# Merged evacuation of the gate and value banks, a tap moved to ScalarE, and more seven-product couples with sums made in place

## The chip, the cores and the metric

The kernel runs on one core of one Trainium2 chip. The metric is the device time of one execution in microseconds (us); lower is better. Each time is the median of several executions. TensorE (PE) does the matrix products, VectorE (DVE) and ScalarE (ACT) do elementwise work, GpSimd (POOL) a little of it, and SyncE (SP) issues nearly all transfers.

## The reference, cut to what matters

Two layers; each is a token mixer (an mLSTM, then an HGRN2) followed by the ConvGLU below, with a norm ahead of each and a residual add behind it. All is float32; 256 tokens, width 2048, inner width 5504.

```python
def conv_glu(hn, w_up, conv_w, conv_b, w_down):
    u = hn @ w_up
    a, v = jnp.split(u, 2, axis=-1)
    s = a.shape[1]
    pad = CONV_W // 2                      # CONV_W = 3
    ap = jnp.pad(a, ((0, 0), (pad, pad), (0, 0)))
    c = conv_b
    for j in range(CONV_W):
        c = c + ap[:, j:j + s] * conv_w[j]
    return (jax.nn.gelu(c, approximate=False) * v) @ w_down
...
    for layer in range(DEPTH):             # DEPTH = 2
        ...
        h = h + mix
        h = h + conv_glu(rmsnorm(h, norm_ffn_g[layer]), ffn_w_up[layer], ...)
    return rmsnorm(h, final_g)
```

## The kernel before

**Products.** Every float32 operand is split in a rounded high part and the rest: ScalarE casts (`wh`, L137), VectorE subtracts (`wl`, L138). A product of a 128x128 block of tokens by a 128x512 block of weights is then three matmuls: high by high, high by low, low by high.

**The feed-forward part** (`ffn`) works in two parts of 22 and 21 blocks of 128 inner channels. First come the "up" chunks, one for each block (kind "fm"): 16 steps of the width, two banks of PSUM, one for the gate half a and one for the value half v; each bank is 512 wide, and the second 256 columns hold the term of the low part of x. `done_up` then evacuates the two banks: for each, ScalarE copies the second half (L355), VectorE adds the first half to it (L356) and multiplies by the norm's row R (L361). VectorE makes the three taps of the convolution (middle tap L1118, side taps L1119 and L1120), ScalarE the Gelu (L1121), VectorE the product with v (L1122), and the result is split into `g` (L1124, L1125).

**The "down" chunks** (kind "st", `squares_by_seven`) take two blocks at a time, a couple, against two column blocks of 512. A plain couple is eight products, 24 matmuls. In a couple listed in `SEVEN` the 2x2 block product is made with seven (Winograd's form): C11, C12, C21 and C22 in four banks of one pool, P1, P6, P7 and P5 in four banks of the other. It needs four sums of token blocks S1 to S4 (`token_sums`, made right after the up chunk) and four sums of weight blocks T1 to T4. After the last seven-product couple `mid` adds P1, P5, P6 and P7 into the residual stream, after the last couple `done` adds the C banks. The down chunks of part 0 are d0 and d1 (columns 0 to 1023 and 1024 to 2047), of part 1 d0 alone, and the rest of part 1 is an ordinary product, d2. A chunk of part 0 has 11 couples, 0 to 10; part 1 has ten and a single block.

**The weights' sums.** While the up chunks run, `prepare` loads the weights of each couple in `STORED`, makes the four sums in three VectorE operations into two other tiles (`weight_sums`, L179, L182, L184; the tiles are `pth` for the weights and `ptl` for the sums), and stores them to a scratch tensor in memory. In the down chunk the sums come back (`T`, L197), and `combine` splits them: `th0` and `th1` by ScalarE (L209), `tl0` and `tl1` by VectorE (L210). There is one buffer each of `th0`, `th1`, `tl0` and `tl1`, and `prepare` uses the same four. A couple in `SEVEN` but not in `STORED` (couple 9 of d0 in part 0) has its sums made on the spot.

**What sets the order.** The kernel is written in program order; the compiling layer simulates a timeline and sorts each engine's instructions by it, and each engine then runs its own list strictly in that order. Transfers of the up chunks and of `prepare` are pinned to program order (`late`). Side work such as `prepare` is a generator that is stepped as products are issued (`side.tick`); a yield of 1.0 is about 1 us of products. `split_squares` makes the operands of a down chunk three pieces ahead of its use, and first steps `prepare` to its end if it isn't there yet. Buffers: 3 of `raw` (loaded weights), 4 of `wh` and `wl`, 3 of `avc`/`T` in the feed-forward part. SyncE issues loads and stores in one queue, in order.

## Time and profile before

| | |
|---|---|
| time of 3 runs | 2391.53, 2390.47, 2388.43 us; median 2390.47 us |
| the profiled execution | span 2388.5 us from its first to its last instruction; the page gives no other time of it |
| PE | 2372.4 us busy (99%), 14614 matmul records |
| DVE | 1944.1 us (81%), 3221 instructions |
| ACT | 1298.8 us (54%) |
| POOL | 189.7 us (8%) |
| transfers | 555.07 MB, mean 232 GB/s |

[...] The up chunks of part 0 of the first layer run from about 383 to 635 us of the span, d0 and d1 from 635 to 745, the up chunks of part 1 to 980, and its down chunks to about 1080. The second layer's feed-forward part has the same stages from 1677 us to the end.

### The profile page before, as it was taken

To read this page: it belongs to the slowest core of one execution; us is meant where nothing else is said; L and a number is where in the kernel's file an instruction comes from. 1 tells how busy PE (TensorE), PEld (TensorE's weight loads), DVE (VectorE), ACT (ScalarE), POOL (GpSimd) and SP (SyncE) were. 2 spreads that over 40 slices of the span, in tenths; PEclk is the share of its full clock that TensorE was granted. 3 is DMA by queue.
4 is the path that set the end of the run, shared out by engine and by line. 5 is a ranking of instruction groups with operands and counts; after the bars stand their busy time and mean duration, and the time that the engine had idled before them with its cause. 6 is when DMAs were issued, how large, how long until landed. Compare 5 with 4: busy or idle time off the path is not lost.

```text
span 2388.5 us, 37988 instructions
## 1 busy us (share of the span) xinstructions
PE 2372.4 (99%) x14614; PEld 2030.4 (85%) x14614; DVE 1944.1 (81%) x3221; ACT 1298.8 (54%) x2013; POOL 189.7 (8%) x240
## 2 busy tenths in 40 slices
PE   9999999999999999999999999999999999999998
PEld 7888888888888888888888888888888888888887
DVE  7766687988887888777888888888889888788874
ACT  7655455454564554555555555555555565454563
POOL 0100000000000000001222222220000000000000
PEclk9999999999999999999999999999999999999999
DMA  8654556988787777755554554545798888677774
GB/s 300 201 180 165 183 178 211 333 294 317 269 293 254 251 239 262 273 194 182 173 171 168 175 177 160 177 166 188 258 325 298 298 281 296 231 249 263 249 266 148
DMA packets 98789, 555.07 MB, mean 232 GB/s; under 512 B 11168, under 2 KB 11680, under 8 KB 50736
## 3 DMA queue, kind: packets, MB, share of 16 engines
q1 hardware_dynamic: 96912, 548.64, 65.6%
q0 software_dynamic: 1120, 3.21, 0.7%
q8 instruction: 114, 1.87, 0.3%
q10 hardware_dynamic: 576, 0.79, 0.1%
q14 instruction: 67, 0.55, 0.1%
HBM read 512.69 MB, written 39.91 MB: 231 GB/s over the span
## 4 chain that ended last, share of the span: by engine, by line
PE 98%; DVE 1%; issue 1%; DMA 0%; ACT 0%; SPq 0%; POOLq 0%; POOL 0%
PE mm L328 37%; PE mm L344 23%; PE mm L332 18%; PE pc L237 12%; PE mm L237 5%; PE pn L776 1%; PE py L1034 1%; PE pd L984 1%; PE pz L405 0%; PE pa L984 0%; DMA raw<-in_w_first 0%; PE S L762 0%; DVE tl L210 0%; PE pz L1055 0%; PE pa L1009 0%
## 5 line engine op out<-in xcount | busy, mean ns | idle before, releaser
L328 PE MATMUL mm<-xt,wh 128*128 128x512 f32 x3776 | 1313.4, 394 | 0.0
L137 ACT CAST wh<-raw 128x1024 fp32r<-128x1024 f32 (+1 forms) x846 | 853.5, 1019 | 693.8 <-PE mm L328 237.9
L138 DVE TENSOR_TENSOR wl<-raw,wh 128x1024 fp32r<-128x1024 f32 (+1 forms) x846 | 1004.7, 1195 | 265.1 <-ACT wh L137 257.6
L332 PE MATMUL mm<-xt,wl 128*128 128x256 f32 x3776 | 1045.9, 278 | 0.0
L328 PEld LDWEIGHTS mm<-xt,wh 128*128 128x128 f32 x3776 | 706.2, 188 | 159.4
L332 PEld LDWEIGHTS mm<-xt,wl 128*128 128x128 f32 x3776 | 709.5, 188 | 4.5 <-issue 0.4
L344 PE MATMUL mm<-wh,xt 128*128 128x512 f32 x1024 | 320.5, 391 | 3.0 <-ACT xt L350 1.3
L344 PEld LDWEIGHTS mm<-wh,xt 128*128 128x128 f32 x1024 | 191.4, 188 | 43.3 <-ACT xt L350 1.7
L344 PE MATMUL mm<-wl,xt 128*128 128x512 f32 x512 | 198.2, 391 | 0.0
L237 PE MATMUL pc<-wh,g 128*128 128x512 f32 x508 | 167.2, 389 | 0.0
L355 ACT COPY b<-mm 128x256 f32<-128x256 f32 x236 | 87.4, 370 | 122.9 <-PE mm L332 122.7
L210 DVE TENSOR_TENSOR tl<-T,th 128x1024 fp32r<-128x1024 f32 x88 | 109.9, 1264 | 38.9 <-ACT th L209 36.7
L209 ACT CAST th<-T 128x1024 fp32r<-128x1024 f32 x88 | 92.7, 1054 | 73.6 <-PE mm L237 43.5
L237 PEld LDWEIGHTS pc<-wh,g 128*128 128x128 f32 x508 | 95.4, 188 | 19.9
L344 PEld LDWEIGHTS mm<-wl,xt 128*128 128x128 f32 x512 | 96.2, 188 | 18.9
L553 POOL TENSOR_TENSOR hm<-hm,u 128x512 f32<-128x512 f32 x8 | 10.4, 1302 | 1150.9 <-DVE u L552 1150.9
L237 PE MATMUL pc<-wl,g 128*128 128x512 f32 x254 | 98.9, 389 | 0.0
L344 PE MATMUL mm<-wh,g 128*128 128x512 f32 x308 | 96.6, 392 | 0.0
L237 PE MATMUL mm<-th,sx 128*128 128x512 f32 x264 | 91.9, 390 | 0.0
L356 DVE TENSOR_TENSOR avc<-mm,b 128x256 f32<-128x256 f32 x172 | 72.0, 418 | 14.7 <-ACT b L355 14.7
L361 DVE TENSOR_TENSOR avc<-avc,R 128x256 f32<-128x256 f32 x172 | 71.9, 419 | 1.6
L976 DVE COPY kq<-QK 128x256 f32<-128x256 f32 x224 | 69.7, 336 | 0.0
(260 smaller groups left out, 2476.7 us busy)
## 6 DMA issues: line engine op xcount, KB each, us to landing
raw<-in_w_up SPq DMA_DIRECT2D x172, 1024.0 KB, 5.5
raw<-in_w_d SPq DMA_DIRECT2D x48, 1024.0 KB, 5.0
raw<-in_w_bq SPq DMA_DIRECT2D x48, 1024.0 KB, 4.9
pth<-in_w_d SPq DMA_DIRECT2D x72, 512.0 KB, 6.7
tscr<-ptl SPq DMA_DIRECT2D x72, 512.0 KB, 4.7
T<-tscr SPq DMA_DIRECT2D x72, 512.0 KB, 5.1
raw<-in_w_d SPq DMA_DIRECT2D x36, 768.0 KB, 5.2
raw<-in_w_ao SPq DMA_DIRECT2D x24, 1024.0 KB, 4.8
```

Of the source, the lines that this page charges most:

```text
L137: pin(act.copy(wh[:, :m], r))
L138: pin(dve.tensor_tensor(wl[:, :m], r, wh[:, :m].bitcast(F32), ALU.subtract))
L209: act.copy(th, t)
L210: dve.tensor_tensor(tl, t, th.bitcast(F32), ALU.subtract)
L237: pe.matmul(ps, a, b, start=id(ps) not in begun, stop=stop and i == 2)
L328: pe.matmul(ps[f], wh[:, c:c + P], x, start=k + kk == 0, stop=False)
L332: pe.matmul(ps[f][:, 0:T], wl[:, c:c + P], x[:, 0:T], start=False, stop=k + kk == ch.nk - 1)
L344: pe.matmul(ps[t], x[:, a + t * P:a + (t + 1) * P], w[:, c], start=st and i == 0, stop=sp and i == 2)
L355: act.copy(b, ps[:, T:2 * T])
L356: dve.tensor_tensor(dst, ps[:, 0:T], b, ALU.add)
L361: dve.tensor_tensor(dst, dst, R, ALU.mult)
L976: dve.tensor_copy(m[:, j].rearrange("k (m p j) -> k m p j", p=2, j=h), blocks(z, h, 0, T))
```

## The change

It has four parts.

1. The up chunk's two banks are one tile of two banks (`banks`). One ScalarE copy takes both second halves (128x512), one VectorE addition both first halves, one VectorE multiplication applies R to both. The pool of four single banks becomes a pool of two such pairs, for all users: in a down chunk P1 and P6 share one tile, P7 and P5 the other.
2. The middle tap with its bias goes from VectorE to ScalarE (an activation of kind Identity).
3. `prepare` loads the weights of a couple into one pair of tiles (`pth` and `ptl` in turn), one couple ahead, and VectorE makes the sums in place in four operations of 128x512 each, so that no second pair of tiles is needed; it then stores them. The tiles then hold T2, T3 (first tile) and T4, T1 (second tile), where before they held T1, T3 and T2, T4.
4. Of the couples, 8 a chunk in d0 and d1 of part 0 and 6 in part 1 have seven products, all of them with stored sums. Before it was 7, 6 and 6, with 6 stored in each. In part 0 the couples are 1, 2, 3, 5, 6, 7, 8 and 9 instead of 1, 2, 4, 5, 7, 8 (and 9 in d0). To save room, the token sum S4 goes into a part of `g` that a seven-product couple doesn't read (part 0) or into a tile of its own (part 1).

```diff
-SEVEN = (1, 2, 4, 5, 7, 8, 9), (1, 2, 4, 5, 7, 8), (1, 2, 4, 5, 7, 8)
-STORED = (1, 2, 4, 5, 7, 8)
+SEVEN = (1, 2, 3, 5, 6, 7, 8, 9), (1, 2, 4, 5, 7, 8)
...
-    psm = ctx.enter_context(tc.tile_pool(name="psm", bufs=4, space=PSUM))
+    psm = ctx.enter_context(tc.tile_pool(name="psm", bufs=2, space=PSUM))
...
+    def banks():
+        return psm.tile([P, 2, 512], F32, tag="mm", name="mm")
+
     def squares_by_seven(ch, fetch, ready):
 
-        psm_ = [psm.tile([P, 512], F32, tag="mm", name="mm") for _ in range(4)]
-        P1, P6, P7, P5 = psm_
+        P1, P6, P7, P5 = psm_ = [ps[:, i] for ps in (banks(), banks()) for i in range(2)]
...
-                sx, t = ch.sums(u), q[2]
-                S1, S3, S2, S4 = ((sx[:, i * P:(i + 1) * P], sx[:, 512 + i * P:512 + (i + 1) * P]) for i in range(4))
-                T1, T3, T2, T4 = (block(t[i // 2], i % 2) for i in range(4))
+                (S1, S3, S2, S4), t = ch.sums(u), q[2]
+                T1, T3, T2, T4 = (block(t[i // 2], i % 2) for i in ((3, 1, 0, 2) if u in ch.stored else range(4)))
...
-            ps = [psm.tile([P, 512], F32, tag="mm", name="mm") for _ in range(2)]
+            both = banks()
+            ps = [both[:, i] for i in range(2)]
...
-    def token_sums(mp, i, a, b, S):
+    def token_sums(mp, i, a, b, S, last=None):
...
+        act.copy(sx[:, 0:m], S[:, 0:m])
+        dve.tensor_tensor(sx[:, m:2 * m], S[:, 0:m], sx[:, 0:m].bitcast(F32), ALU.subtract)
+        if last:
+            act.copy(last[0], S[:, m:512])
+            dve.tensor_tensor(last[1], S[:, m:512], last[0].bitcast(F32), ALU.subtract)
...
     def prepare(mp, todo, period, finished):
 
-        yield 24.0
-        for src, dst in todo:
-            r, T = ([mp.tile([P, 1024], F32, tag=f"{n}{i}", name=f"p{n}") for i in range(2)] for n in ("th", "tl"))
-            for i in range(2):
-                late(r[i], src[:, i * 1024:(i + 1) * 1024])
-            yield 9.0
-            yield from weight_sums(*r, *T)
-            for i in range(2):
-                nc.sync.dma_start(dst[i], T[i])
-            yield max(1.0, period - 14.0)
+        loaded = []
+
+        def load(i):
+            if i < len(todo):
+                n = ("th", "tl")[i % 2]
+                r = [mp.tile([P, 1024], F32, tag=f"{n}{j}", name=f"p{n}") for j in range(2)]
+                for j in range(2):
+                    late(r[j], todo[i][0][:, j * 1024:(j + 1) * 1024])
+                loaded.append(r)
+
+        yield 18.0
+        load(0)
+        for i, (_, dst) in enumerate(todo):
+            yield period / 2
+            load(i + 1)
+            B11, B22, B21, B12 = (loaded[i][j // 2][:, j % 2 * 512:(j % 2 + 1) * 512] for j in range(4))
+            for x, y, out in ((B12, B22, B22), (B12, B11, B12), (B11, B22, B11), (B21, B11, B21)):
+                dve.tensor_tensor(out, x, y, ALU.subtract)
+                yield period / 8
+            for j in range(2):
+                nc.sync.dma_start(dst[:, j * 1024:(j + 1) * 1024], loaded[i][j])
         finished.append(True)
...
-                fm_scaled(ps[0], R, a)
-                fm_scaled(ps[1], R, v)
+                av = avc[:, 0:2 * T].rearrange("p (a b) -> p a b", a=2)
+                act.copy(av, ps[:, :, T:2 * T])
+                dve.tensor_tensor(av, ps[:, :, 0:T], av, ALU.add)
+                dve.tensor_tensor(av, av, R.unsqueeze(1).broadcast_to([P, 2, T]), ALU.mult)
                 cw = [col("conv_w", (layer * 3 + w) * FT + f) for w in range(3)]
-                dve.tensor_scalar(c, a, cw[1], col("conv_b", layer * FT + f), ALU.mult, ALU.add)
+                act.activation(c, a, AF.Identity, bias=col("conv_b", layer * FT + f), scale=cw[1])
...
-                side.push(prepare(box["mp"], todo, (nf * 10.4 - 24.0) / len(todo) - 1.5, finished))
+                side.push(prepare(box["mp"], todo, (nf * 10.4 - 26.0) / len(todo), finished))
...
-                chunks.append(two(w_d1[layer], 2, None, SEVEN[1]))
+                chunks.append(two(w_d1[layer], 2, None, SEVEN[0]))
```

The changed program keeps 846 `wh` casts and 846 `wl` subtractions. It has 13363 matmul instructions where the one before has 13381, 3075 VectorE instructions for 3221, 1975 ScalarE instructions for 1933, and 723 transfers in SyncE's queue for 675.

More of the change, by code (lines that the diff above doesn't have):

```diff
@@ L195, in raw @@
                     kept[u] = [temporary(ch.pool, "T") for _ in range(2)]
-                    for t, src in zip(kept[u], ch.stored[u]):
-                        nc.sync.dma_start(t, src)
+                    for i, t in enumerate(kept[u]):
+                        nc.sync.dma_start(t, ch.stored[u][:, i * 1024:(i + 1) * 1024])
             return raws.get(u)
@@ L346, in stream @@
                     k += 1
-            ch.done(ps)
+            ch.done(both if ch.paced else ps)
     def split(dst, src, gcol, pin=lambda ins: ins):
@@ L524, in slot @@
         return where.tile([P, 2 * T], F32R, tag=f"yt{j}", name=f"{name}{j}")
-    def token_sums(mp, i, a, b, S):
-        sx = mp.tile([P, 1024], F32R, tag=f"sx{i}", name="sx")
+    def token_sums(mp, i, a, b, S, last=None):
+        m = 384 if last else 512
+        sx = mp.tile([P, 2 * m], F32R, tag=f"sx{i}", name="sx")
         for i, (x, y, op) in enumerate(((a[:, P:T], b[:, P:T], ALU.add), (a[:, P:T], a[:, 0:P], ALU.subtract),
@@ L532, in token_sums @@
             dve.tensor_tensor(S[:, i * P:(i + 1) * P], x, y, op)
-        act.copy(sx[:, 0:512], S)
-        dve.tensor_tensor(sx[:, 512:1024], S, sx[:, 0:512].bitcast(F32), ALU.subtract)
-        return sx
+        act.copy(sx[:, 0:m], S[:, 0:m])
[3 more added lines that the diff above has]
+            dve.tensor_tensor(last[1], S[:, m:512], last[0].bitcast(F32), ALU.subtract)
+        return [(sx[:, i * P:(i + 1) * P], sx[:, m + i * P:m + (i + 1) * P]) for i in range(m // P)] + ([last] if last else [])
     def pair(src, nk, c0, x, sums, norm, seven, late=False):
@@ L1098, in ffn @@
         stack = ExitStack()
-        box = dict(n=3 * len(STORED) * layer)
+        box = dict(n=(2 * len(SEVEN[0]) + len(SEVEN[1])) * layer)
         chunks, pairs = [], []
@@ L1127, in go @@
                 if i % 2 and i // 2 in seven:
-                    SX[i // 2] = token_sums(mp, seven.index(i // 2), box["c"], c, avc[:, 0:2 * T])
+                    n = seven.index(i // 2)
+                    if seven is SEVEN[0]:
+                        z = GT[i - 1][:, P:T], GT[i - 1][:, T + P:2 * T]
+                    else:
+                        if n % 3 == 0:
+                            box["s4"] = mp.tile([P, 768], F32R, tag=f"sx{len(seven) + n // 3}", name="s4")
+                        z = tuple(box["s4"][:, (n % 3 * 2 + j) * P:(n % 3 * 2 + j + 1) * P] for j in range(2))
+                    SX[i // 2] = token_sums(mp, n, box["c"], c, avc[:, 0:2 * T], z)
                 box["c"] = c
@@ L1137, in prep @@
                     begin()
-                side.push(prepare(box["mp"], todo, (nf * 10.4 - 24.0) / len(todo) - 1.5, finished))
+                side.push(prepare(box["mp"], todo, (nf * 10.4 - 26.0) / len(todo), finished))
             for i in range(nf):
-                chunks.append(Chunk("fm", w_up[layer, f0 + i], KT, norm.x, done_up(f0 + i, i, GT, SX, SEVEN[2 * part]),
+                chunks.append(Chunk("fm", w_up[layer, f0 + i], KT, norm.x, done_up(f0 + i, i, GT, SX, SEVEN[part]),
                                     prep if i == 0 else None,
@@ L1145, in two @@
                 ch = pair(src, nf, c0, lambda k: GT[k], lambda u: SX[u], norm, seven)
-                for u in STORED:
+                for u in seven:
                     ch.stored[u] = tscr[box["n"]]
@@ L1152, in two @@
                 return ch
-            chunks.append(two(w_d0[layer][:, f0 * 1024:(f0 + nf) * 1024], 0, nxt if part else None, SEVEN[2 * part]))
+            chunks.append(two(w_d0[layer][:, f0 * 1024:(f0 + nf) * 1024], 0, nxt if part else None, SEVEN[part]))
             if part:
@@ L1268, in build @@
     mscr = nc.dram_tensor("mscr", (64, T), F32, kind="Internal").ap()
-    tscr = nc.dram_tensor("tscr", (6 * len(STORED), 2, P, 1024), F32, kind="Internal").ap()
+    tscr = nc.dram_tensor("tscr", (4 * len(SEVEN[0]) + 2 * len(SEVEN[1]), P, 2048), F32, kind="Internal").ap()
     with tile.TileContext(nc, schedule_with_timeline_sim=True) as tc:
```

## The prediction

> **What bounds the kernel now.** I read the page's head first, then what TensorE waited for, then the chain that ended last, and last the stretches of one feed-forward part.

> ```profile
> span 2388.5 us, 37988 instructions
> ...
> PE 2372.4 (99%) x14614; PEld 2030.4 (85%) x14614; DVE 1944.1 (81%) x3221; ACT 1298.8 (54%) x2013; POOL 189.7 (8%) x240
> ...
> PEclk9999999999999999999999999999999999999999
> ```
> ```profile
> PE mm L237 <- DVE tl L210: 0.6, 2, 0.3
> ```
> ```profile
> 2317.31 5.44 PE pc L237 x24
> ```
> ```profile
> 383.00:635.00 252.00, 252.00 (x1449) 220.00 (x1449) 220.03 (x368) 131.19 (x195) 0.70 (x1) 1.00 0.81 292
> 635.00:750.00 115.00, 114.69 (x510) 94.62 (x509) 94.25 (x102) 67.11 (x76) 7.09 (x4) 1.00 0.79 280
> ```

> TensorE is busy 99% of the span at full clock. In the seven-product chunks (L237) it waited 0.6 us in all, for `tl`. So the time is a sum of matmuls, and only two things move it: how many there are, and any new wait in TensorE's list. The chain's row gives the price of one 128x512 matmul: 5.44 / 24 = 0.2267 us. The rows by stretch (columns: time, then busy time of PE, weight loads, DVE, ACT, POOL, clock, transfer share, GB/s) show how thin the cover is: in the up chunks of part 0 (383 to 635) VectorE is busy 87%, in d0 and d1 (635 to 750) 82%.

> **Part 1 and 2, evacuation and tap.**

> ```profile
> L356 DVE TENSOR_TENSOR avc<-mm,b 128x256 f32<-128x256 f32 x172 | 72.0, 418 | 14.7 <-ACT b L355 14.7
> L361 DVE TENSOR_TENSOR avc<-avc,R 128x256 f32<-128x256 f32 x172 | 71.9, 419 | 1.6
> ...
> L1121 ACT ACTIVATE avc<-avc 128x256 f32<-128x256 f32 x86 | 35.7, 415 | 42.3 <-DVE avc L1120 42.1
> L1118 DVE TENSOR_SCALAR avc<-avc,pp 128x256 f32<-128x256 f32 x86 | 34.9, 406 | 0.0
> ...
> L559 DVE TENSOR_TENSOR hm<-hm,pc 128x512 f32<-128x512 f32 x32 | 20.9, 676 | 0.1
> ```

> VectorE loses 72.0 + 71.9 + 34.9 = 178.8 us and gains 172 operations of 0.676 us (the row of a 512-wide addition from PSUM), 116.3 us: 62 us less, 0.73 us a chunk. ScalarE takes 86 taps of about 0.415 us, 36 us more, and the merged copy saves a little. Neither is on the path: TensorE has a second pair of banks while one is evacuated, and a chunk of products lasts 252 / 22.7 = 11.1 us. On the path this is 0; without that cover it would be one copy and one addition a chunk, 86 x 1.3 = 112 us, which no wait of the profile suggests. The order is another matter: see below.

> **Part 3, the sums in place.**

> ```profile
> L179 DVE TENSOR_TENSOR ptl<-pth 128x1024 f32<-128x1024 f32 x36 | 44.0, 1223 | 26.5 <-DMA pth<-in_w_d 22.7 <-issue 3.6
> ...
> L184 DVE TENSOR_TENSOR ptl<-pth,ptl 128x512 f32<-128x512 f32 x36 | 24.6, 683 | 0.0
> ```
> ```profile
> SPq L583 <- DVE ptl L179: 80.1, 20, 7.3
> ```
> ```profile
> raw<-in_w_up SPq DMA_DIRECT2D x172, 1024.0 KB, 5.5
> ```

> Before, 36 couples cost 1.223 + 2 x 0.683 = 2.59 us each; now 44 cost 4 x 0.683 = 2.73 us: 120 for 93 us, 27 us more on VectorE. In part 0 that is 16 for 12, +12.6 us, against 22 x 0.73 = 16.0 us saved there: VectorE stays near 87%. Loading one couple ahead takes away the 22.7 us it idled for `pth`; off the path, so 0. In SyncE's queue 16 loads, 16 stores and 16 reads back of 512 KB are added. A store waits for VectorE (80.1 us in all before) and the `raw` loads behind it wait too; their cover is the two other `raw` buffers, 2 x 5.5 us of products, against a landing of 5.5 us. I cost it at 0; with the cover gone, one landing, 5.5 us.

> **Part 4, the products.** Three more couples a layer have seven products: 2 layers x 3 x 3 = 18 matmuls, 18 x 0.2267 = **-4.1 us**. TensorE has nothing else to give.

> **The new waits.** In a run of seven-product couples `th0`, `th1`, `tl0`, `tl1` have one buffer each, so a couple's sums are split only when TensorE has read the last one's.

> ```profile
> 693.27 0.39 PE L237 MATMUL mm<-th,sx 128*128 128x512 f32 x1
> ```
> ```profile
> 693.70 1.05 ACT L209 CAST th<-T 128x1024 fp32r<-128x1024 f32 x1 [0.27 <-PE mm L237]
> ```
> ```profile
> 653.98 2.36 DVE L210 TENSOR_TENSOR tl<-T,th 128x1024 fp32r<-128x1024 f32 x2 [3.61 <-ACT th L209]
> ```
> ```profile
> L210 DVE TENSOR_TENSOR tl<-T,th 128x1024 fp32r<-128x1024 f32 x88 | 109.9, 1264 | 38.9 <-ACT th L209 36.7
> ```

> The cast starts 0.43 us after the start of the last matmul that reads (693.27 to 693.70) and takes 1.05; a subtraction takes 1.22 and the second of a pair ends 2.36 - 1.22 = 1.14 later. Counted from the start of the last read of `th0`, with 0.03 for each hand-over: `th0` at 1.51, `tl0` at 2.77, `th1` at 2.57, `tl1` at 3.91. The built programs' order tells how many matmuls stand in between. Before, at least 20 stand between the last read of a tile and the first matmul of the next couple that needs the new `tl` (4.5 us): no wait. Two things end this. Tiles shared by P1/P6 and P7/P5 keep P1 of the next couple behind P6 of this one, and P7 behind P5, so fewer matmuls can be brought forward; and couples 5 to 9 follow each other. In the changed program's TensorE order, couple 9 follows couple 8 like this (last reads of 8, first of 9):

> ```
> 3654 mm_6215<-th0_6440   3655 pc_6219<-tl1_6445   3656 pc_6219<-th1_6444
> 3657 mm_6215<-th0_6483 [waits ACT]   3658 mm_6215<-tl0_6484 [waits DVE]   3659 mm_6215<-th0_6483
> 3660 mm_6216<-th1_6487 [waits ACT]   3661 pc_6219<-th1_6487   3662 mm_6216<-tl1_6488 [waits DVE]
> ```

> Couple 10 has been used up as filler ahead of 3654. Matmul 3657 has its place 3 x 0.2267 = 0.68 us after 3654 and starts at 1.51: wait 0.83. 3658 could start at 1.74 and starts at 2.77: 1.03. 3662 has its place four later, 3.68, and starts at 3.91: 0.23. Together 2.1 us, in d0 and d1 of both layers (the order is the same): **+8.4 us**.

> Couples 2 to 3 of d0: 6 matmuls stand between; the first of 3 waits 1.51 - 1.36 = 0.15, its `th1` matmul 2.57 - 1.74 = 0.83: 1.0 us, twice: **+2.0 us**. The other neighbours (3 to 5, 5 to 6, 6 to 7, 7 to 8, and part 1) have 11 to 34 before `th0` and 13 or more before `tl0` is needed, 2.9 us against 2.77: 0.

> From d0 to d1, VectorE's list after `tl1` of couple 9 (3.91) is: five evacuations, `tl0` of d1's couple 1, one more, `wl` of d1's couple 1, `tl1`, and the addition that frees P7/P5.

> ```profile
> 688.64 0.68 DVE L551 TENSOR_TENSOR hm<-hm,mm 128x512 f32<-128x512 f32 x1
> ...
> 689.23 0.68 DVE L548 TENSOR_TENSOR u<-u,mm 128x512 f32<-128x512 f32 x1
> ...
> 695.41 2.29 POOL L554 TENSOR_TENSOR hm<-hm,u 128x512 f32<-128x512 f32 x1
> ```

> An evacuation takes 0.60 (688.64 to 689.23), so `wl` ends at 3.9 + 6 x 0.60 + 2 x 1.14 = 9.8. TensorE wants it 21 matmuls after 3662, at 8.7: wait 1.1; the freed bank comes at 9.8 + 1.14 + 0.6 = 11.5, wanted 5 matmuls later at 10.9: 0.6. Together 1.7 us, twice: **+3.4 us**. POOL's additions come behind that. From d1 to the up chunks the same list leaves 1.8 us of room: 0.

> **Sum.** -4.1 + 8.4 + 2.0 + 3.4 = +9.7 us. Against the profiled span 2388.5 that is 2398.2; the median of the runs stands 2.0 above that span, so I forecast **2400 us**, 0.4% slower.

> **The transfers, as a bound.**

> ```profile
> T<-tscr SPq DMA_DIRECT2D x72, 512.0 KB, 5.1
> ```
> ```profile
> DMA to landing us min/median/max: 3.3/5.1/7.8
> ```
> ```profile
> 720.00:725.00 5.00, 2.16 (x3) 1.00 0.99 387
> ```
> ```profile
> 425.00:435.00 10.00, 10.00 (x60) 8.73 (x59) 9.34 (x15) 5.21 (x8) 0.00 (x0) 1.00 0.92 347
> ```

> A seven-product couple loads 768 + 2 x 512 KB, 1.84 MB in 21 x 0.2267 = 4.76 us, 386 GB/s, as much as the best five microseconds of d1 (387). A run of five at 347 GB/s takes 26.5 us for 23.8: 2.7 us late, in four chunks 10.7 us, less what the plain couples give back. I take 0, since d0 and d1 together need 35.7 MB in 109 us, 328 GB/s. The second `T` tile of couple 9 is loaded only once `tl0` of couple 8 frees its buffer, at the latest 11 matmuls (2.5 us) ahead of 3654, so 4.0 us before its cast could start at 1.5: at a landing of 5.1 it's up to 1.1 us late, at 7.8 up to 3.8, four times 4.4 or 15. I take 0, because that `tl0` may end earlier. [...]

> **Rivals.**

> *Only the waits from 8 to 9 show* (d0 to d1 and 2 to 3 covered, as before's own 0.6 us speaks for): 2390.5 - 4.1 + 8.4 = 2395, no measurable change.

> *Transfers bind in the long runs*: the rows above speak for it, the mean against it. 2400 + 11 = 2411.

> *The matmuls saved come through and no wait does*: 2390.5 - 4.1 = 2386.4, not slower. It needs the waits to sum to under 4.1 us, that is 8 to 9 under 1.0 us each. Against it stands the row of a cast that starts only after the read; for it, that VectorE sheds 62 us and could be earlier everywhere else.

> *The clock falls after the new waits.* It's at full in every slice, and where TensorE stops for good the row shows less:

> ```profile
> 2379.00:2388.50 9.50, 0.87 (x4) 0.38 (x2) 3.80 (x8) 2.67 (x4) 0.68 (x2) 0.69 0.60 221
> ```

> Six us of half clock behind each of four stops would cost 4 x 3 = 12 us: 2412. The longest single wait is 1.0 us. [...]

> **Chances.** The forecast as worked out 0.48; only 8 to 9, 0.20; transfers 0.20; no wait 0.05; clock 0.03; something in the up chunks not seen 0.04. What a measurement can tell from no change is about 0.2%, 4.8 us: slower beyond 2395.3 is then 0.75, within 0.20 (the case of 2395), faster 0.05. The range is 2391 to 2414: below, the case of 2395 with half its waits; above, the case of late transfers. The forecast's own range is 2396 to 2405.

> **What would show it.** Right: TensorE 4 us less of matmuls in L238, and in its waits some 14 us in L238 for `th0`/`th1` (ACT) and `tl` (DVE), at four places of about 2 us near 690 and 740 and their like in the second layer; VectorE's total some 20 us less; clock full. Wrong: no such waits, or waits in the up chunks for `wl`, or casts there and in d0 released by transfers of `T`.

## The result, and the profile after

The changed kernel takes 2429.4 us (median of 5 runs, 2426.5 to 2432.4) against the 2390.5 us of before; run beside each other the ratio is 1.0163, with a 95% interval of 1.0150 to 1.0175. It is 1.6% slower. I had forecast 2400 us, so the direction was right and 29 us were missing. The profiled execution of the changed kernel took 2427.9 us, its span is 2426.2 us, 37.7 us longer than the span shown of before.

The page's head, with the shares of the chain that ended last, then what TensorE waited for (behind the arrow the releaser, that is, the engine and tile that ended the wait; then total us, times, longest us):

```profile
span 2426.2 us, 38067 instructions
...
PE 2386.3 (98%) x14596; PEld 2030.4 (84%) x14596; DVE 1933.8 (80%) x3075; ACT 1349.0 (56%) x2055; POOL 194.2 (8%) x240
...
PE 83%; DMA 7%; DVE 6%; issue 2%; ACT 1%; SPq 0%; POOL 0%; POOLq 0%; ACTq 0%; DVEq 0%
```
```profile
PE mm L238 <- ACT th L208: 10.3, 10, 1.8
PE pd L1000 <- issue: 6.1, 3, 2.5
PE mm L238 <- DVE tl L209: 4.2, 5, 1.1
PE pc L238 <- ACT wh L136: 3.3, 3, 2.3
PE mm L238 <- ACT wh L136: 1.6, 3, 0.7
PE pc L238 <- ACT th L208: 1.4, 2, 0.7
```

The 18 matmuls are gone (14614 to 14596). But TensorE is idle 39.9 us of the span (2426.2 - 2386.3) where it was idle 16.1, and its busy time rose by 13.9 us although it has less to do, because part of it ran at half clock (three stretches of 3.4 us at a clock of 0.50), and because a matmul's record (0.39 us and more) is longer than the distance to the next start (0.2267 us), so that a part of each wait counts as busy. In the chain TensorE had 98% before; now it has 83%, and transfers and VectorE have 13%. In line 238, the seven-product products, the waits for `th`, `tl` and `wh` sum to 20.8 us. And one row has nothing to do with these chunks: 6.1 us ahead of the small `pd` products of the second mixer, with no releaser.

One row of ScalarE's waits, before and after, shows that its casts of `th` now wait for transfers of `T`:

```profile
ACT th L209 <- DMA T<-tscr: 7.1, 6, 2.0
```
```profile
ACT th L208 <- DMA T<-tscr: 21.4, 14, 3.8
```

The stretches tell where the time went. First before, then after, each with d0 and d1 of the first layer, the second mixer, and d0 and d1 of the second layer (columns as in the prediction: time, then busy time of PE, weight loads, DVE, ACT, POOL, clock, transfer share, GB/s):

```profile
635.40:747.10 111.70, 111.39 (x492) 91.71 (x491) 91.29 (x98) 65.44 (x74) 7.09 (x4) 1.00 0.79 278
...
1093.00:1679.40 586.40, 582.79 (x4988) 499.54 (x4988) 508.93 (x1003) 325.49 (x606) 142.96 (x179) 1.00 0.51 174
...
1925.00:2036.60 111.60, 111.34 (x492) 91.61 (x491) 91.38 (x98) 65.25 (x74) 7.08 (x4) 1.00 0.79 279
```
```profile
636.50:761.80 125.30, 116.21 (x482) 89.92 (x481) 94.74 (x104) 73.19 (x86) 3.00 (x2) 0.99 0.83 299
...
1107.90:1702.00 594.10, 585.90 (x4988) 501.19 (x4987) 507.46 (x1003) 326.55 (x606) 146.55 (x179) 1.00 0.51 172
...
1947.60:2073.40 125.80, 115.14 (x482) 90.08 (x481) 92.82 (x100) 71.63 (x83) 3.01 (x2) 0.99 0.82 294
```

d0 and d1 take 13.6 and 14.2 us more, 27.8 together, with 9 matmuls fewer each; the mixer takes 7.7 us more for the same products; the rest of the span adds 2.2 (0.9 at the end of the first up chunks, 1.1 in the last chunk). I added up the distances between starts of matmuls in d0 and d1, less the 0.2267 us that one is worth. Both layers together have 32.4 us of idle or slowed time there:

| place in d0 and d1, both layers | us |
|---|---|
| couple 1 of d0, waiting for `th` and for the `wh` behind it | 4.1 |
| couple 3 of d0, waiting for `th` | 6.2 |
| half clock right behind it | 3.2 |
| couple 8 to 9, four times | 8.9 |
| d0 to d1, twice | 4.5 |
| later waits for `T` or `raw` | 5.6 |

Less the 4.1 us of matmuls saved, that is 28.3, against the 27.8 by which the two stretches grew.

### The profile page after: what moved, and what is told of

Its sections match the earlier page's. It is cut to its first block, busy times and chain, and to the rows that moved or that the text cites. A ratio compares the mean times of both kernels' runs of the same rounds, so it can differ in the third digit from the quotient of the medians.

```text
span 2426.2 us, 38067 instructions
## 1 busy us (share of the span) xinstructions
PE 2386.3 (98%) x14596; PEld 2030.4 (84%) x14596; DVE 1933.8 (80%) x3075; ACT 1349.0 (56%) x2055; POOL 194.2 (8%) x240
## 4 chain that ended last, share of the span: by engine, by line
PE 83%; DMA 7%; DVE 6%; issue 2%; ACT 1%; SPq 0%; POOL 0%; POOLq 0%; ACTq 0%; DVEq 0%
PE mm L329 31%; PE mm L345 21%; PE mm L333 16%; PE pc L238 7%; PE mm L238 4%; DVE wl L137 2%; DMA T<-tscr 2%; DMA pth<-in_w_d 2%; DMA ptl<-in_w_d 1%; DVE tl L209 1%; ACT th L208 1%; PE pn L792 1%; DMA raw<-in_w_d 1%; PE py L1050 1%; PE pd L1000 1%
## 5 line engine op out<-in xcount | busy, mean ns | idle before, releaser
L209 DVE TENSOR_TENSOR tl<-T,th 128x1024 fp32r<-128x1024 f32 x100 | 120.1, 1221 | 60.8 <-ACT th L208 60.5
L238 PE MATMUL pc<-wh,g 128*128 128x512 f32 x488 | 163.3, 391 | 3.4 <-ACT wh L136 3.3
L208 ACT CAST th<-T 128x1024 fp32r<-128x1024 f32 x100 | 102.8, 1050 | 98.1 <-PE mm L238 56.3
L238 PE MATMUL mm<-th,sx 128*128 128x512 f32 x300 | 107.9, 397 | 10.6 <-ACT th L208 10.3
L238 PEld LDWEIGHTS pc<-wh,g 128*128 128x128 f32 x488 | 91.9, 188 | 24.1 <-ACT wh L136 5.1
L238 PE MATMUL pc<-wl,g 128*128 128x512 f32 x244 | 95.6, 392 | 0.1
L1136 ACT ACTIVATE avc<-avc,pp 128x256 f32<-128x256 f32 x86 | 51.7, 601 | 51.4 <-DVE avc L1134 51.0
L238 PEld LDWEIGHTS mm<-th,sx 128*128 128x128 f32 x300 | 56.9, 190 | 26.3 <-ACT th L208 14.3
L597 DVE TENSOR_TENSOR ptl<-ptl 128x512 f32<-128x512 f32 x88 | 60.4, 686 | 23.2 <-DMA ptl<-in_w_d 22.9
L597 DVE TENSOR_TENSOR pth<-pth 128x512 f32<-128x512 f32 x88 | 60.3, 685 | 21.2 <-DMA pth<-in_w_d 15.0
## 6 DMA issues: line engine op xcount, KB each, us to landing
raw<-in_w_up SPq DMA_DIRECT2D x172, 1024.0 KB, 6.3
raw<-in_w_bq SPq DMA_DIRECT2D x48, 1024.0 KB, 5.0
T<-tscr SPq DMA_DIRECT2D x88, 512.0 KB, 5.5
raw<-in_w_d SPq DMA_DIRECT2D x40, 1024.0 KB, 5.2
raw<-in_w_ao SPq DMA_DIRECT2D x24, 1024.0 KB, 4.8
pth<-in_w_d SPq DMA_DIRECT2D x44, 512.0 KB, 8.0
ptl<-in_w_d SPq DMA_DIRECT2D x44, 512.0 KB, 7.8
```

Source lines behind the costliest of these rows:

```text
L208: act.copy(th, t)
L209: dve.tensor_tensor(tl, t, th.bitcast(F32), ALU.subtract)
L238: pe.matmul(ps, a, b, start=id(ps) not in begun, stop=stop and i == 2)
L597: dve.tensor_tensor(out, x, y, ALU.subtract)
L1136: act.activation(c, a, AF.Identity, bias=col("conv_b", layer * FT + f), scale=cw[1])
```

## The experiments

Four theories stood against each other, under the letters that the expectations use. **O**: the order of TensorE's list, with tiles shared by two banks, makes the waits (the prediction's). **L**: the preparation of the weights' sums in part 0 ends too late, so SyncE issues the first loads of `T` late. **D**: the transfers can't feed runs of seven-product couples. **M**: the merged banks or the sums in place are slow by themselves. For the mixer's waits there were **F** (TensorE waits for its next block of instructions) and **C** (the change itself causes them). Every kernel is compared with the kernel before on the same chip, 2389.6 to 2390.4 us in these comparisons.

What suggested L, in rows. SyncE's first load of `T` before and after:

```profile
621.65 3.32 SPq L197 DMA_DIRECT2D T<-tscr  x2
```
```profile
635.88 0.32 SPq L196 DMA_DIRECT2D T<-tscr  x1
```

ScalarE and TensorE of the changed kernel at the start of d0 (start, time, then in brackets the idle time before and its releaser):

```profile
644.60 1.04 ACT L208 CAST th<-T 128x1024 fp32r<-128x1024 f32 x1 [1.86 <-DMA T<-tscr]
...
647.02 0.58 ACT L1132 COPY avc<-mm 128x512 f32<-128x512 f32 x1
...
661.33 2.21 ACT L208 CAST th<-T 128x1024 fp32r<-128x1024 f32 x2 [2.51 <-DMA T<-tscr]
```
```profile
645.70 0.50 PE L238 MATMUL pc<-th,g 128*128 128x512 f32 x1 [0.67 <-ACT th L208]
...
662.42 0.50 PE L238 MATMUL mm<-th,sx 128*128 128x512 f32 x1 [1.79 <-ACT th L208]
...
696.35 0.50 PE L238 MATMUL mm<-th,sx 128*128 128x512 f32 x1 [0.67 <-ACT th L208]
...
697.60 0.50 PE L238 MATMUL mm<-tl,sx 128*128 128x512 f32 x1 [0.76 <-DVE tl L209]
```

d0 starts at about 636, and the first `T` is asked for at 635.9, 14 us later than before. ScalarE, in order, sits in front of the cast of couple 1, and behind that cast wait the weights' casts and the evacuation of the last up chunk (647.02; it was at 635.29 before). The three buffers of `T` are the up chunks' too, and the last up chunk holds one of them, so the first `T` of couple 3 is asked for only at 655.4, when VectorE has read one of couple 2; it lands (has arrived) 5.8 us later, and its cast at 661.33 is what couple 3 waits for. The last two rows are the place from couple 8 to 9.

**The sums prepared faster** (early_sums).

```diff
-  prepare(box["mp"], todo, (nf * 10.4 - 26.0) / len(todo), finished)
+  prepare(box["mp"], todo, min(10.4, (nf * 10.4 - 26.0) / len(todo)), finished)
```

> Edit: the changed kernel, with the sums of the weights in part 0 prepared faster, a couple every 10.4 us of products instead of 14.3 (sixteen couples end about one up chunk earlier). Theory L (the preparation ends too late): T of couple 1 reaches d0 earlier, so the waits at the start of d0 (about 2 us for th of couple 1, 3.1 us for th of couple 3) and the half clock behind the second (1.7 us) go in both layers, 2 x 6.8 = 13.6 us; in the built order couple 7 to 8 of d0 now has three matmuls between its reads like 8 to 9, which costs 1.6 us twice: 2429 - 13.6 + 3.2 = about 2419. Theory O (the order of TensorE's list is the cause): these waits stay, 2429 + 3 = 2432. Theory D (the transfers bind): the up chunks now ask for 2.1 MB of sums beside 2.1 MB of weights in 11.1 us, 380 GB/s against a best of 387, so the up chunks of part 0 get waits for raw or wl and nothing is gained, 2429 or more.

Measured 2425.1 us, 4.3 less than the changed kernel; single runs overlap (2420.9 to 2428.7, and 2426.5 to 2432.4), so the trace has to tell. Its first load of `T`, a wait that the changed kernel doesn't have, and the five microseconds around that wait:

```profile
622.86 0.33 SPq L196 DMA_DIRECT2D T<-tscr  x1
```
```profile
1807.95 0.38 PE L333 MATMUL mm<-xt,wl 128*128 128x256 f32 x1 [0.88 <-DVE wl L137]
```
```profile
1805.00:1810.00 5.00, 4.12 (x24) 3.37 (x24) 5.00 (x8) 4.28 (x6) 0.00 (x0) 1.00 0.91 375
```

Theory L holds for the start of d0: `T` is asked for 13 us earlier, the waits of couples 1 and 3 are gone in both layers (the first wait of d0 is now at 676), and d0 with d1 are 3.2 and 5.8 us shorter, with the new waits from 7 to 8 in them. In the second layer the up chunks got four such waits for `wl` of 0.7 to 0.9 us and became 5.8 us longer, so that layer gained nothing. Theory D had named such waits, but not for what the trace shows: in the 4 us ahead of each, VectorE was busy for 3.96 us or more, and ScalarE's casts waited for `raw` for 0.8 us in that whole stage. So these waits are VectorE's, which has the sums between its other work, and not the transfers'.

**The old couples** (old_couples).

```diff
-SEVEN = (1, 2, 3, 5, 6, 7, 8, 9), (1, 2, 4, 5, 7, 8)
+SEVEN = (1, 2, 4, 5, 7, 8), tuple([1, 2, 4, 5, 7, 8])
```

> Edit: the changed kernel, with six seven-product couples a chunk (1, 2, 4, 5, 7, 8) in d0 and d1 of part 0 and in part 1, all with stored sums; merged evacuation, the tap on ScalarE and the sums in place stay. 24 matmuls more than the changed kernel, 5.4 us. Theory L and theory O both: no wait in d0 and d1 is left but 1 us at d1's start, so the time is before's plus 6 matmuls (1.4 us), 2392; if the mixer's 7.7 us (TensorE's small products waiting on nothing that the profile shows, and a half clock) come from the merged banks, 2400. Theory M (merged banks or the sums in place are themselves slow): 2405 or more, with waits in d0 and d1 for th or for banks.

Measured 2395.9 us (2394.4 to 2398.1). 33.5 us of the 39 went with two of the eight couples, although 5.4 us of matmuls came back: d0 and d1 take 112.6 and 113.2 us. The first `T` is asked for at 626.8, and at d0's start no wait for `th` is left, only one of 0.6 us for `wl` in the second layer. The time lies 4 us above the 2392 of theories L and O; the next runs say what that is.

**Merged evacuation and the tap alone, on the kernel before** (merged_alone).

```diff
-    psm = ctx.enter_context(tc.tile_pool(name="psm", bufs=4, space=PSUM))
+    psm = ctx.enter_context(tc.tile_pool(name="psm", bufs=2, space=PSUM))
-        psm_ = [psm.tile([P, 512], F32, tag="mm", name="mm") for _ in range(4)]
+        P1, P6, P7, P5 = psm_ = [ps[:, i] for ps in (banks(), banks()) for i in range(2)]
...
+                act.copy(av, ps[:, :, T:2 * T])
+                dve.tensor_tensor(av, ps[:, :, 0:T], av, ALU.add)
+                dve.tensor_tensor(av, av, R.unsqueeze(1).broadcast_to([P, 2, T]), ALU.mult)
...
+                act.activation(c, a, AF.Identity, bias=col("conv_b", layer * FT + f), scale=cw[1])
```

> Edit: the kernel before with parts 1 and 2 of the change alone (merged banks and evacuation, tap on ScalarE); sums and couples as before. As predicted: nothing on the path, 2390. Rival: the mixer between the two feed-forward parts loses its 7.7 us here too, because its chunks' banks are now freed in pairs, 2398.

Measured 2399.4 us, ratio 1.0044 (1.0029 to 1.0059). So these parts cost 9.3 us by themselves, and not in the mixer (586.9 us, before 586.4). d0 with d1 take 4.1 us more in each layer. TensorE where d0 gives way to d1 in this kernel, and ScalarE's first copy of `mid` in this kernel and before:

```profile
691.80 0.51 PE L239 MATMUL mm<-wh,g 128*128 128x512 f32 x1 [1.58 <-ACT wh L137]
693.39 0.51 PE L239 MATMUL pc<-wh,g 128*128 128x512 f32 x1 [1.09 <-DVE hm L562]
```
```profile
688.95 0.58 ACT L549 COPY u<-mm 128x512 f32<-128x512 f32 x1
```
```profile
679.42 0.59 ACT L546 COPY u<-mm 128x512 f32<-128x512 f32 x1
```

`mid` copies P1 at 688.95 instead of 679.42, and VectorE's first addition from these banks begins at 687.99 instead of 681.80: P1 now shares its tile with P6. So the evacuations that free the banks of d1 fall together with d1's first splits, TensorE waits twice, 2.7 us by these rows, and runs at half clock behind that (from 694.39 us, for 3.4 us).

**Banks of their own in the changed kernel** (single_banks).

```diff
-        P1, P6, P7, P5 = psm_ = [ps[:, i] for ps in (banks(), banks()) for i in range(2)]
+        P1, P6, P7, P5 = psm_ = [psm.tile([P, 512], F32, tag="mm", name="mm") for _ in range(4)]
...
-                act.copy(av, ps[:, :, T:2 * T])
-                dve.tensor_tensor(av, ps[:, :, 0:T], av, ALU.add)
-                dve.tensor_tensor(av, av, R.unsqueeze(1).broadcast_to([P, 2, T]), ALU.mult)
+                fm_scaled(ps[0], R, a)
+                fm_scaled(ps[1], R, v)
```

> Edit: the changed kernel with part 1 undone: four banks of their own in the pool, each evacuated by a copy, an addition and a multiplication; the tap stays on ScalarE, the sums in place and the 8, 8 and 6 couples stay. Theory O (shared tiles keep the couples' matmuls in line): in the built order 11 and 7 matmuls stand between the reads from couple 8 to 9 instead of 3, so the four waits of 2.3 us there fall to 0 in d1 and 0.7 in d0, a gain of 7.8 us, about 2421; the waits at the start of d0 stay. Theory D: the couples wait for T or raw instead, and the gain is under 3 us. If the mixer's 7.7 us come from the shared tiles, they go too, 2413.

Measured 2409.8 us, 19.6 less than the changed kernel. d0, d1 and the up chunks behind them (their products overlap, so I take them together) are 3.0 and 5.0 us shorter. These 8.0 agree with the 7.8 of theory O by luck. As it said, the waits from 8 to 9 in d1 are gone. But in d0 the stretch from couple 5 to couple 9 has 14.3 us of idle or slowed time in both layers, where the changed kernel has 7.7; its longest wait, 1.9 us at 697.9, ends with a cast that waited for `T`:

```profile
696.84 1.04 ACT L208 CAST th<-T 128x1024 fp32r<-128x1024 f32 x1 [3.17 <-DMA T<-tscr]
```

The start of d0, where theory O expected no change, has 8.1 us for 13.8, and the waits from d0 to d1 are gone. The mixer is 10.5 us shorter, more than I expected; idle_half below shows that 8.2 us can go there by the place of the instructions alone, with the tiles as they are.

**Parts 2 and 3 alone** (single_old: the last two edits together, banks of their own and the old couples).

> Edit: banks of their own and six couples a chunk (1, 2, 4, 5, 7, 8) everywhere, all with stored sums; so the kernel before with parts 2 and 3 alone (tap on ScalarE, sums in place), and without couple 9 of d0, 6 matmuls more than before (1.4 us). If parts 2 and 3 are free as predicted: 2391 to 2393, and the 4 us that the run with old couples and merged banks stands above it are the merged banks' price. If the sums in place cost by themselves: 2395 or more, with waits in d0.

Measured 2391.3 us, ratio 1.0004 (0.9995 to 1.0014). With twelve couples in part 0 the tap on ScalarE and the sums in place cost nothing, and theory M falls for them. The merged banks cost 4.6 us there (2395.9 - 2391.3), but not where they did in merged_alone: by the two profiles 2.4 us lie ahead of the first feed-forward part and 2.0 in the second mixer, while d0 and d1, from their first to their last matmul, take 112.4 and 112.9 us against 112.5 and 112.4. In merged_alone the last seven-product couple of d0 is couple 9, here it is couple 8; the 4.1 us a layer were seen only with couple 9.

**The tap back on VectorE** (tap_back).

```diff
-                act.activation(c, a, AF.Identity, bias=col("conv_b", layer * FT + f), scale=cw[1])
+                dve.tensor_scalar(c, a, cw[1], col("conv_b", layer * FT + f), ALU.mult, ALU.add)
```

> Edit: the changed kernel with part 2 undone, the middle tap is again VectorE's. As predicted: nothing, 2427 to 2431. Rival (ScalarE's list holds the last up chunk's evacuation behind its casts, and the tap of 0.60 us lengthens it): the first waits of d0 shrink and the time falls by 2 us a layer, 2425.

Measured 2436.6 us: 7.2 us slower than the changed kernel. Both expectations missed, in sign too. In its row of waits:

```profile
PE pc L238 <- ACT wh L136: 7.2, 5, 2.8
...
PE mm L238 <- DVE tl L209: 5.9, 10, 1.1
```

Those rows were 3.3 and 4.2. d0 with d1 grew by 4.2 and 5.2 us, in all their parts: 3.0 us of it at d0's start (couples 1 to 3), 1.8 from couple 5 to 9 of d0, 1.6 from d0 to d1, and 3.2 in d1, both layers together. So part 2 was worth 7.2 us in this kernel; why isn't shown. That VectorE has too much to do at d0's start doesn't explain it: there, in the first layer, it idles 2.2 and 2.4 us (from 640.9 and 644.3) for ScalarE's casts of `th`. The order of the instructions is another too, since the compiling layer sorts them anew; couple 7 to 8 of d0 now has waits of 0.84 and 0.72 us, as in early_sums, which the changed kernel hasn't.

**The warm-up made longer** (idle_more and idle_half).

```diff
-    for i in range(90):
+    for i in range(154):      # idle_more; range(122) in idle_half
```

> Edit: the changed kernel with 64 more of the small warm-up matmuls at the very start, nothing else (at most 1.5 us longer there; they shift the place of each later instruction in TensorE's stream by 128). Theory F (the mixer's waits in front of its 128x32 products, 6.1 us in three places, are TensorE waiting for its next block of instructions, each ends 2.3 us after a transfer of 16384 bytes of instructions began): at another place in the block they shrink to 3 us or less, and with them the half clock behind the longest; 2422 to 2425. Theory C (they come from the change in the kernel): three waits of about 2 us stay, 2429 to 2431.

Measured 2432.8 us (2426.5 to 2441.3), and the three waits stayed, 5.9 us in all, behind the same products of their groups. As theory F was put there, that is a miss. Then I counted: the trace shows each warm-up step as two matmuls and two weight loads, so 64 more are 256 instructions, and the transfers of instructions went from 114 to 115 blocks of 16384 bytes. The records of the changed kernel, 14596 matmuls and 14596 weight loads, are 256 for each of its 114 blocks; so, by this estimate, the shift was one whole block, and left every later product where it had been in its block.

> Edit: the changed kernel with 32 more warm-up matmuls at the very start (the trace shows each as two matmuls and two weight loads, so 128 instructions, half of a 16384-byte block at 64 bytes each by the count of blocks in the trace). The run with 64 more moved TensorE's stream by exactly one block, and its three waits of 2 us stayed in the same products (behind number 119, 121 and 125 of their groups, as without). Theory F (the wait is for the next block of instructions, when a block ends inside the 130 small products): half a block moves the end of the blocks out of these groups, so the waits go or fall on other groups, in all less than 4 us instead of 6.1; about 2424. Theory C (these waits belong to the products themselves): they stay behind the same products, 2429 to 2432.

Measured 2426.5 us. By the starts of matmuls the mixer takes 586.0 us instead of 594.2, as much as before the change, and the row for `pd` is gone. What it has instead is at the start:

```profile
PE idle L1196 <- issue: 2.6, 1, 2.6
```

The start became 3.5 us longer, 2.6 of it by that wait at the warm-up itself, and d0 with d1 came out 2.2 and 2.7 us longer, so the sum hardly moved. Theory F is what the two runs show: a whole block leaves the waits in their places, half a block removes them.

**Mended versions** (single_early: single_banks with early_sums; single_seven: single_banks with seven couples in d0 and d1, a pace of 13.7; single_mid: single_banks, the preparation started 16 earlier, a pace of 13.7).

```diff
-SEVEN = (1, 2, 3, 5, 6, 7, 8, 9), (1, 2, 4, 5, 7, 8)
+SEVEN = (1, 2, 4, 5, 7, 8, 9), (1, 2, 4, 5, 7, 8)      # single_seven only
...
-        yield 18.0
+        yield 2.0                                        # single_mid only
...
-  prepare(box["mp"], todo, (nf * 10.4 - 26.0) / len(todo), finished)
+  prepare(box["mp"], todo, min(11.7, (nf * 10.4 - 26.0) / len(todo)), finished)   # 10.4 in single_early
```

> Edit: both the banks of their own (part 1 undone) and the faster preparation (a couple every 10.4 us of products). Theory L: on top of the 2410 of the banks alone the waits at d0's start go (in the banks' run 2 to 3 us a layer), and the up chunks of part 0 get waits for wl of up to 6 us in one layer, as in the run with the faster preparation: 2404 to 2412. Theory D (transfers bind in d0): the waits of 0.7 to 1.9 us near 692 to 700 stay, since the order leaves 0.6 us.

> Edit: banks of their own, seven couples (1, 2, 4, 5, 7, 8, 9) in d0 and d1 of part 0 instead of eight, all with stored sums, a couple prepared every 13.7 us of products; tap on ScalarE and sums in place stay. 12 matmuls more than the changed kernel, 6 fewer than before (1.4 us). Theory L with the shared banks gone: the preparation ends a chunk ahead of d0, the order leaves no wait, and no run of couples is longer than three: 2389 to 2393. Theory D: 7, 8, 9 still ask for 386 GB/s and wait for T, 2395 or more.

> Edit: banks of their own, eight couples as in the change, the preparation started 16 us of products earlier and a couple every 13.7 us (so it ends about a chunk before d0 and asks for 330 GB/s instead of 380 beside the up chunks). Theory L: no waits in the up chunks and none for couples 1 and 3 of d0; what is left in d0 and d1 is the transfers (waits for T and raw near 690 to 700, 2 to 4 us a layer) less 4.1 us of matmuls: 2393 to 2401. Rival (TensorE falls into the slower rhythm of 0.353 us for a pair in the up chunks, as in the two runs before this one, without waiting): 2401 to 2407.

Measured 2406.3, 2401.0 and 2407.9 us. The first is inside what was expected, but by luck in part (8.0 us of it are the slow rhythm below, which its expectation hadn't), the second 8 us above it (a time that theory D had named, but with hardly a wait for `T`), the third 0.9 above its rival's range. Few waits are left in single_seven: 1.0 us in the up chunks and 3.3 us from d0 to d1. What is left is a slower rhythm. The same hundred microseconds of up chunks in the kernel before and in single_seven:

```profile
800.00:900.00 100.00, 100.00 (x579) 87.48 (x578) 84.70 (x141) 50.48 (x76) 0.00 (x0) 1.00 0.73 253
```
```profile
800.00:900.00 100.00, 100.00 (x568) 86.67 (x567) 82.32 (x143) 54.74 (x88) 0.00 (x0) 1.00 0.72 254
```

Busy all the time, full clock, the same transfers, and 11 matmuls fewer: a pair of a 512-wide and a 256-wide matmul takes 0.3533 us instead of 0.3467. Summed over the up chunks of both layers this costs 8.0 us in single_early, 10.1 in single_seven and 14.4 in single_mid, 0.4 in the changed kernel and 0.2 before. Often the slow rhythm begins at a wait for `wl` (at 572 in single_seven, at 511 in single_mid), but it also begins without one, so what sets it stays open. In d0 of single_early the waits near 692 to 700 stay, as theory D said: ScalarE's cast at 694.93 waited 2.67 us for `T`.

**A shift of the kernel before** (before_shift).

```diff
-    for i in range(90):
+    for i in range(58):
```

> Edit: the kernel before with 32 fewer warm-up matmuls at the very start, nothing else (half a block of instructions less ahead of everything). Theory F: the two waits of 1.4 and 1.5 us behind small products of the mixer, which the kernel before has too, go or move; the start may lose up to 2 us because the first products find the array colder or come earlier. Expected 2386 to 2390, at most 0.1% faster. If the waits stay behind the same products, theory F falls for this kernel.

Measured 2388.65 us over 11 runs against 2390.36 over 15: ratio 0.9990 (0.9981 to 0.9999). The waits ahead of `pd` fell from 2.6 to 0.9 us. In the kernel before the first products do run slower: its trace has 59 warm-up matmuls at work in the 1.00 us from 2.50 us of the span, and 72 in the 0.70 us from 3.55. The shifted kernel is the only version that comes out below the kernel before, by 0.1%; none with more seven-product couples does.

## Why the prediction was right and wrong

**What bounds the kernel, and part 4.** Right: TensorE's list sets the time, and 18 matmuls went, 4.1 us.

**The waits from couple 8 to 9.** Right, down to the parts: I worked out 0.83 and 1.03 us for d0, the trace has 0.84 and 1.03 at 696, and 0.85 and 1.03 at 756 in d1 (distances between starts, less 0.2267; the idle time in the rows above, 0.67 and 0.76, is less, since a record lasts longer than that). Instead of the 0.23 for `tl1` each stop costs another 0.11 us or so in the next weight load (from 697.60 to the next start at 697.94 it is 0.34 us instead of 0.2267), so the four sum to 8.9 for 8.4. The cause named, tiles shared by two banks, is shown for d1, where these waits are gone with banks of their own (single_banks). In d0 a wait for `T` takes their place there, so for d0 that run decides nothing.

**Couples 2 to 3.** Not seen as predicted: the wait there is 3 us and not 1.0, and it is for the transfer of `T`, which hides what the order alone would cost.

**d0 to d1.** Place right, size 4.5 for 3.4 us, but mostly not by the cause that I gave. VectorE's list ends 0.39 us (`wl`) and 0.46 us (the freed bank) of it in the first layer, and none in the second. The larger waits, 0.95 and 2.42 us, end with ScalarE's cast of `wh`, which stands behind a cast of `th` that waited for `T`, 0.34 us in the first layer and 1.82 in the second:

```profile
2014.85 1.04 ACT L208 CAST th<-T 128x1024 fp32r<-128x1024 f32 x1 [1.82 <-DMA T<-tscr]
2015.80 0.61 ACT L136 CAST wh<-raw 128x512 fp32r<-128x512 f32 x1
```
```profile
2016.46 0.50 PE L238 MATMUL pc<-wh,g 128*128 128x512 f32 x1 [2.26 <-ACT wh L136]
```

A second cause that I hadn't seen is that `mid` can't start on P1 until P6 is done: merged_alone, without the late sums, has waits here too, and is 4.1 us a layer longer with the half clock behind them. I had used the shared tile for the order of matmuls and not for the order of evacuations.

**Parts 1 and 2 at nothing.** This step failed. VectorE did shed what I said (178.8 us became 58.8 + 59.1 = 117.9; I had 116.3), though its total fell by 10.3 us and not by the 20 that I named as a sign. But the price of part 1 isn't in the up chunks, where I looked for its cover: it is where other chunks use the same pool: 9.3 us on the kernel before, 8.2 of them in d0 and d1. The tap's move wasn't nothing either: 7.2 us to the good in the changed kernel, for a reason that stays open, and with part 3 nothing that could be measured in single_old. It costs ScalarE 0.60 us each where I took 0.415:

```profile
L1136 ACT ACTIVATE avc<-avc,pp 128x256 f32<-128x256 f32 x86 | 51.7, 601 | 51.4 <-DVE avc L1134 51.0
```

**Part 3 and SyncE's queue at nothing.** This is the step that failed most: I gave it 0, or 5.5 us with the cover gone, and it is 13.5 us (4.1 + 6.2 + 3.2 in the table above). early_sums, with the sums ready earlier, has none of these waits. VectorE's total was right (60.4 + 60.3 us for the sums; I had 120), and the mean of 86% in the up chunks too. (The 22.7 us that it idled for the weights didn't go: they are 22.9 + 15.0 now, off the path.) The time at which the preparation ends was never worked out, and it could have been: a step of products is 0.65, each yield is rounded up to it, so a couple takes 6.5 + 4 x 1.95 = 14.3, and sixteen with the 18 ahead of them 247, where part 0 has 22 x 10.4 = 229. Before it was 24 + 12 x 16.25 = 219. So two couples are left over when d0 begins, and their loads, sums and stores stand in SyncE's queue ahead of the first `T`. With twelve couples (old_couples) it is 244, one is left over, and no wait for `T` showed, so it takes more than a late end by itself. A mean over the stage couldn't show this; the place where the stage ends does.

**The transfers at nothing.** The rival was right in kind: I named the second `T` of a late couple, 4.4 or 15 us over four times, and casts in d0 released by transfers of `T` as a sign of being wrong. Waits for `T` or `raw` beside those at d0's start sum to 5.6 us, and the 1.82 us from d0 to d1 come on top. No run changes the transfers alone, so this part rests on the trace. In d1, the issue of a `T` tile of couple 7 and its time to landing, ScalarE's cast of it and TensorE's wait:

```profile
736.58 1.46 SPq L196 DMA_DIRECT2D T<-tscr  x2
```
```profile
DMA to landing us min/median/max: 6.9/6.9/6.9
```
```profile
743.61 1.04 ACT L208 CAST th<-T 128x1024 fp32r<-128x1024 f32 x1 [1.74 <-PE pc L238]
```
```profile
744.71 0.50 PE L238 MATMUL mm<-th,sx 128*128 128x512 f32 x1 [0.98 <-ACT th L208]
```

The cast's wait is put down to TensorE, but the tile asked for at 736.58 landed 6.9 us later, at 743.5, and the cast began at 743.61: so it is the transfer that it waited for, at a time when couples 7, 8 and 9 load together.

**The clock, a chance of 0.03.** This rival came true beside the others. What I set against it was the longest single wait, which was to be 1.0 us. The trace has waits of up to 2.5 us, and three half-clock stretches of 3.4 us, each 1.7 us lost; the last section has what TensorE lacked ahead of them.

**The mixer.** No step of the prediction looked there, since the change touches no line of it. It lost 7.7 us, and idle_half shows that all of it goes with half a block of instructions.

In sum: -4.1 and +8.9 + 4.5 stood in my sum, as -4.1 and +8.4 + 3.4 (the last for another cause in the main); the 2.0 of couples 2 to 3 stood there for a place where 6.2 was lost to something else. Not in it were the waits behind the late preparation (13.5), the transfers (5.6), the mixer (7.7) and 2.2 elsewhere. All together that is 38.3 us, for the 37.7 measured.

## What to carry to other kernels

Side work that is paced by a count has an end: work out that end, with its rounding, and compare it with the moment at which its result is first wanted, before any share of busy time is used as cover. Before that work is made faster, see which engine has room for it where it runs: in early_sums VectorE had none. When a buffer is merged to save instructions, look at every other user of the same pool, and ask for each who waits for the merged tile's last writer. And where a change shifts a long list of instructions, compare a stage that it doesn't touch: if that moved too, the change has to be judged without it, as idle_half and before_shift do here.

## What the runs showed of the hardware

```profile
660.51:663.92 3.41, 0.96 (x3) 0.48 (x3) 1.52 (x2) 2.47 (x3) 0.00 (x0) 1.00 0.62 234
663.92:667.33 3.41, 3.41 (x9) 2.63 (x8) 1.47 (x2) 0.70 (x2) 0.00 (x0) 0.50 0.65 211
1493.36:1496.77 3.41, 0.90 (x103) 0.79 (x90) 2.92 (x6) 1.93 (x8) 0.00 (x0) 1.00 0.65 197
1496.77:1500.18 3.41, 3.41 (x16) 2.96 (x16) 1.38 (x6) 0.57 (x3) 1.07 (x2) 0.50 0.51 214
2005.36:2008.77 3.41, 1.97 (x8) 1.09 (x7) 2.93 (x3) 2.09 (x2) 0.00 (x0) 1.00 0.75 240
2008.77:2012.18 3.41, 3.37 (x15) 2.47 (x14) 3.21 (x6) 1.85 (x3) 0.00 (x0) 1.00 0.72 225
```

I laid such windows over the feed-forward parts in the 14 profiles of this case and summed what TensorE lacked in each, with 0.2267 us as the worth of a 512-wide matmul and, as an estimate, half of it for a 256-wide one. Of the 5769 windows at full clock, all 10 that lacked 2.3 us or more were followed by half clock, 2 of the 5 that lacked 2.06 to 2.13 us were, and none of the others, which lacked 2.01 us or less. In the mixers 6 more windows were followed by half clock; what they lacked is less certain, since the worth of their small products is. Ahead of the stretch at 663.92 two waits, of 1.79 and 0.66 us, lay in one window, while a wait of 2.4 us that straddles two windows (at 2014 to 2016 in the changed kernel) was followed by full clock.

**Three waits of TensorE came with transfers of instructions.** In the changed kernel's second mixer a group of 130 small products takes 1.8 us (1223.34 to 1225.10); three such groups stop near their end for 2.0 to 2.7 us, each until 2.2 to 2.4 us after a transfer of 16384 bytes of instructions began. The profile calls this idle time "issue", 6.1 us in all. With 256 instructions more ahead of them (idle_more) three waits stayed, 5.9 us, behind the same products; with 128 more (idle_half) the row is gone. That TensorE waited there for its own instructions is my reading of these two runs.

**The same matmuls at full clock ran in two rhythms**, 0.3467 and 0.3533 us a pair, as the rows of 800 to 900 us show (579 and 568 matmuls), and each kernel kept to one for the whole 100 us. It decided whether the mended versions could come near the kernel before, and what sets it wasn't found.
